# The state-space branch without GpSimd arithmetic, the gates' sigmoid in place, and the branch's tables begun seven steps later

## The chip, the core and the metric

The kernel runs on one core of a Trainium2 chip. The core has five engines that run side by side and wait for each other by semaphores: TensorE (PE; its weight loads are PEld), VectorE (DVE), ScalarE (ACT), GpSimd (POOL) and SyncE (SP). SP only issues transfers here; POOL issues some too. Each engine takes its instructions strictly in the order in which the program gives them, so an instruction that waits holds up all that stand behind it on its engine. The metric is the device time of one execution in microseconds.

## The reference, cut to what matters

One layer of a hybrid decoder for 1024 prompt tokens and 64 sample tokens (1088 columns in all; everything is fp32). The start of the layer is what the change touches:

```
h = rms_norm(x, norm_attn_g)
u, q_lat, kv_lat, k_rope, g_a, g_b = split(h @ w_in)        # 512, 384, 256, 32, 1024, 1024 columns
lb, bb = ssm_discretize(lam, log_dt, b)                     # 32 groups x 64 complex states
y, h_last = ssm_scan(u, h0, lb, bb, c, d)                   # h[t] = lb*h[t-1] + bb u[t];  y = Re(c h) + d u
z = gelu(y);  a_out = z * sigmoid(z @ w_glu)
b_out = latent attention (q_lat, kv_lat, k_rope)
x = x + (sigmoid(g_a)*(a_out @ w_branch_a) + sigmoid(g_b)*(b_out @ w_branch_b)) @ w_out
x = x + swiglu ffn(x);  x = x + gated per-layer embedding(x)
```

## The kernel before, in words

**Products.** Activations are stored transposed, 128 channels by 1088 tokens. Each fp32 product is made of three passes: both factors are split into a high and a low part, and `mm3` multiplies high by high, high by low and low by high. A tile of 128 output channels takes eight steps (one for each 128 input channels); a step is nine matmuls, three passes over three column chunks `CH`. A tile's three PSUM buffers are called `d`; there are six of them, so tile n+2 may begin only when tile n has been read out (`tag="d", bufs=6`).

**Weights.** `w_split` brings one unit of eight 128x128 blocks: SP loads `wr` (two buffers), ACT makes the high part `wh` (line 189), DVE the low part `wl` (line 190), and then SP is given the next `wr` load, which must wait until ACT and DVE have read the buffer. This is done at the first step of each tile, for the tile after it.

**Order of the work.** In `body`, the tiles of `w_in` come in this order: two tiles of `u`, which run with the norm's sums of squares (`sum_squares`) while x arrives; two more tiles of `u`; eight gates for `gbS` (called b0 to b7 here); eight for `gaS` (a0 to a7); two tiles of `kv`; one of `k_rope`; three of `q`. After its last step a tile is evacuated: `ev_gate` multiplies by the token's norm factor `Rb` on DVE (`gt`, line 402), takes the sigmoid on ACT (line 404) and stores by a transfer that POOL issues; `ev_u` does the like for `u`.

**Side work.** Everything else of this part is in generators that `tick` advances by one stage after each step: a stage is issued, and `yield n` says that the next comes n steps later. Two are spawned after the first two tiles: the rest of `stats` (token sums on PE, line 273; the inverse root `Rt` in eleven small DVE operations, lines 249 to 254; nine transposes on PE, line 288; `Rb` on ACT, line 290), five steps on; and `ssm_all`, `SW0` steps on. `ssm_all` runs `ssm_tables` (angles, exponentials, powers and the matrices `BB`, nearly all on DVE, some on POOL), then `ssm_block` four times (8 groups each). A block has these stages, with the steps between them in `WT`: `X` and `Y` (products of tables); `kp` in two halves (PE line 601, ACT line 603, sixteen transfers `M<-kp` on SP, line 605) with the transposes of `Y`; `Tc`, `Ts`, `rho`; `v` (PE line 638 in three groups that share two PSUM buffers, ACT line 639); the rotated scan (lines 648 to 671, DVE alone, ending in `Hp` and `fin`); `yb` (PE lines 680 and 681 in three groups, ACT line 682); and `ssm_tail`, whose gelu (line 702) comes much later. POOL does one of the two products in `X`, `Y`, `Tc` and `Ts`, and makes `rho`.

**Buffers.** All [128, 1088] tiles come from an arena of 38 slots: `S.free` puts a slot at the end of a list and `S.get` takes the first. A new tile so waits for the last reader of the slot's tile before; `v` and one `go` of each block have the slots of the two `kp`.

Of the kernel before, what the change touches and what calls it, by code (L numbers as in the profile page):

```python
# [14 lines left out]
AF = mybir.ActivationFunctionType  # L15
ALU = mybir.AluOpType
# [8 lines left out]
NT = SEQ + NS  # L25
# [16 lines left out]

N_SLOTS = 38
WRB = 2
SW0 = 4
WT = (8, 1, 7, 4, 9, 3, 1, 17, 11)
PVLAG = 3
WQ0 = 7
WS = 1
# [73 lines left out]
def body(ctx, tc, I, O):  # L123
    nc = tc.nc
    V, A, G, PE, SP = nc.vector, nc.scalar, nc.gpsimd, nc.tensor, nc.sync
# [87 lines left out]
    def spawn(gen, wait=0):  # L213
        side.append([gen, wait])
# [15 lines left out]
    S = Arena(sb, N_SLOTS)  # L230
# [73 lines left out]
    def sum_squares(k, x, acc):  # L304
        if k < 2:
            A.activation(acc[k], x, AF.Square)
        else:
            s = S.get([128, NT], name="sq")
            A.activation(s, x, AF.Square)
            (V if k % 2 == 0 else G).tensor_tensor(acc[k % 2], acc[k % 2], s, op=ALU.add)  # L310
            S.free(s)

    gaS = T(dr, [8, 128, NT], name="gaS")
# [27 lines left out]
    acc = [S.get([128, NT], name="acc") for _ in range(2)]  # L341
# [10 lines left out]
    Bab = S.get([128, 2, 32, 16], name="Bab")  # L352
# [45 lines left out]
    def ev_gate(m, dst):  # L398
        def ev(ps):
            t = S.get([128, NT], name="gt")  # L400
            for c, (c0, c1) in enumerate(CH):
                V.tensor_tensor(t[:, c0:c1], ps[c][:, :c1 - c0], Rb[:, c0:c1], op=ALU.mult)
            o = S.get([128, NT], name="go")
            A.activation(o, t, AF.Sigmoid)
            G.dma_start(dst[m], o)
            S.free(t, o)
        return ev

    def u_store(m, src):
# [18 lines left out]
    Cab = S.get([128, 2, 32, 16], name="Cab")  # L428
# [3 lines left out]
    def ssm_tables():  # L432
# [4 lines left out]
        def tiny(dt=F32):  # L437
            tn[0] += 1
            if dt is F32:
                return tp[(tn[0] - 1) // 32][:, (tn[0] - 1) % 32, :]  # L440
            return T(cp, [128, 32], dt, "tr")

        def tt(a, b, op, out=None):
            o = tiny() if out is None else out
            V.tensor_tensor(o, a, b, op=op)
            return o
# [48 lines left out]
        t1h = tiny()  # L495
        V.tensor_scalar(t1h, tot, 3072.0, 3072.0, op0=ALU.add, op1=ALU.subtract)
        t1l = tt(tt(tt(tt(s1, t1h, ALU.subtract), s2, ALU.add), s3, ALU.add), rest, ALU.add)

        b3 = [128, 32, 33]
        jb = jmul[:, None, :].to_broadcast(b3)  # L500
        ph = S.get(b3, name="ph")
# [6 lines left out]
            V.tensor_scalar(kk, ph, MAGIC, MAGIC, op0=ALU.add, op1=ALU.subtract)  # L508
            V.tensor_tensor(ph, ph, kk, op=ALU.subtract)

        G.tensor_tensor(ph, jb, t1h[:, :, None].to_broadcast(b3), op=ALU.mult)
        kk2 = S.get(b3, name="kk2")
        G.tensor_tensor(kk2, jb, t1l[:, :, None].to_broadcast(b3), op=ALU.mult)
        yield 3
        wrap()
        yield 1
# [3 lines left out]
        ph2 = S.get(b3, name="ph2")  # L520
        V.tensor_scalar(ph2, ph, 0.25, None, op0=ALU.add)
        V.tensor_scalar(kk2, ph2, MAGIC, MAGIC, op0=ALU.add, op1=ALU.subtract)
        G.tensor_tensor(ph2, ph2, kk2, op=ALU.subtract)
        yield 2
        A.activation(st, ph, AF.Sin, scale=TWO_PI)
        A.activation(ct, ph2, AF.Sin, scale=TWO_PI)
# [5 lines left out]
        pm, Pr, Pi = pw[:, 0], pw[:, 1], pw[:, 2]  # L532
        Prs, Pin, PiS = pw2[:, 0], pw2[:, 1], pw2[:, 2]
# [20 lines left out]
        frb = fr[:, :, None].to_broadcast(b16)  # L554
        f2b = f2[:, :, None].to_broadcast(b16)
        BB = S.get([128, 2, 32, 16], name="BB")
        tmp = S.get([128, 2, 32, 16], name="tmp")
        V.tensor_tensor(BB[:, 0], Bab[:, 0], frb, op=ALU.mult)
        G.tensor_tensor(tmp[:, 0], Bab[:, 1], f2b, op=ALU.mult)
        V.tensor_tensor(BB[:, 0], BB[:, 0], tmp[:, 0], op=ALU.add)  # L560
        G.tensor_tensor(BB[:, 1], Bab[:, 1], frb, op=ALU.mult)
        V.tensor_tensor(tmp[:, 1], Bab[:, 0], f2b, op=ALU.mult)
        V.tensor_tensor(BB[:, 1], BB[:, 1], tmp[:, 1], op=ALU.subtract)
        S.free(tmp, Bab, tp)
# [3 lines left out]
    def ssm_block(q):  # L568
        g0 = 8 * q
        gs = slice(g0, g0 + 8)  # L570
        Pr, Prs, Pin, PiS, pm, BB, st, ct = (SM[k] for k in ("Pr", "Prs", "Pin", "PiS", "pm", "BB", "st", "ct"))
# [5 lines left out]
        bx = [128, 4, 9, 16]  # L577
        for hf in range(2):
            hs = slice(g0 + 4 * hf, g0 + 4 * hf + 4)
            X2 = S.get(bx, name="X2")  # L580
            V.tensor_tensor(X[hf], Cab[:, 0, hs, None, :].to_broadcast(bx), Prs[:, hs, :, None].to_broadcast(bx), op=ALU.mult)
            G.tensor_tensor(X2, Cab[:, 1, hs, None, :].to_broadcast(bx), Pin[:, hs, :, None].to_broadcast(bx), op=ALU.mult)
            V.tensor_tensor(X[hf], X[hf], X2, op=ALU.add)
            S.free(X2)
        Y = S.get([128, 8, 8, 16], name="Y")
        Y2 = S.get([128, 8, 8, 16], name="Y2")
        by = [128, 8, 8, 16]
        G.tensor_tensor(Y, BB[:, 0, gs, None, :].to_broadcast(by), Pr[:, gs, 0:8, None].to_broadcast(by), op=ALU.mult)
        V.tensor_tensor(Y2, BB[:, 1, gs, None, :].to_broadcast(by), PiS[:, gs, 0:8, None].to_broadcast(by), op=ALU.mult)
        V.tensor_tensor(Y, Y, Y2, op=ALU.add)  # L590
        S.free(Y2)
        yield WT[0] + (WQ0 if q == 0 else 0)
        M1 = S.get([128, 8, 128], name="M1")
        Mi = S.get([128, 8, 128], name="Mi")
        for hf in range(2):
# [14 lines left out]
            for i in range(4):  # L610
                PE.transpose(p[:, i * 128:(i + 1) * 128], Y[:, 4 * hf + i].rearrange("p s c -> p (s c)"), ident)
            A.activation(Mi[:, 4 * hf:4 * hf + 4, :], p.rearrange("p (g c) -> p g c", g=4), AF.Copy)
            if WS & 2 and hf == 0:
                yield 1
        S.free(Y)
        yield WT[1]
        Tc = S.get([128, 8, 8, 16], name="Tc")
        Ts = S.get([128, 8, 8, 16], name="Ts")
        t1 = S.get([128, 8, 8, 16], name="t1")
        t2 = S.get([128, 8, 8, 16], name="t2")  # L620
        Ac, As = (x[:, gs, 9:17, None].to_broadcast(by) for x in (ct, st))
        Bc, Bs = (x[:, gs, None, 17:33].to_broadcast(by) for x in (ct, st))
        G.tensor_tensor(Tc, Ac, Bc, op=ALU.mult)
        V.tensor_tensor(t1, As, Bs, op=ALU.mult)
        V.tensor_tensor(Tc, Tc, t1, op=ALU.subtract)
        G.tensor_tensor(Ts, As, Bc, op=ALU.mult)
        V.tensor_tensor(t2, Ac, Bs, op=ALU.mult)
        V.tensor_tensor(Ts, Ts, t2, op=ALU.add)
        rho = S.get([128, 8, 128], name="rho")
        G.memset(rho, 0.0)  # L630
        G.tensor_tensor(rho[:, :, 1:128], rho[:, :, 1:128], pm[:, gs, 8:9].to_broadcast([128, 8, 127]), op=ALU.add)
        yield WT[2]
        v = S.get([128, 8, NCHK], name="v")
        for g in range(0, 8, 3):
# [7 lines left out]
        S.free(Mi)  # L642
        yield WT[3]
        f3 = lambda x: x.rearrange("p g a b -> p g (a b)")
# [27 lines left out]
        S.free(v, Tc, Ts, t1, t2, rho, Gs)  # L672
        yield WT[4]
        yb = S.get([128, 8, NCHK], name="yb")
        for g in range(0, 8, 3):
            n = min(3, 8 - g)
            p = m1()
            for i in range(n):
                o = p[:, i * NCHK:(i + 1) * NCHK]
# [5 lines left out]
        S.free(ug, M1, Hp, X)  # L685
        spawn(ssm_tail(q, yb), WT[5])
        yield WT[6]

    def ssm_tail(q, yb):
        for t in range(8):  # L690
            SP.dma_start(yS[q, t].rearrange("c g j -> c g j"), yb[t * 16:(t + 1) * 16])
        S.free(yb)
        yield WT[7]
        y = S.get([128, 8, NCHK], name="y")
        for g in range(8):
            SP.dma_start(y[g * 16:(g + 1) * 16], yS[q, :, :, g, :].rearrange("t c j -> c t j"))
        u = S.get([128, 8, NCHK], name="u")
        SP.dma_start(u, uS[q].rearrange("p (s j) -> p s j", s=8))
        yield WT[8]
        V.scalar_tensor_tensor(y, u, ssm_d[:, q:q + 1], y, op0=ALU.mult, op1=ALU.add)  # L700
        z = S.get([128, NT], name="z")
        A.activation(z.rearrange("p (j s) -> p s j", s=8), y, AF.Gelu_apprx_tanh)
        SP.dma_start(zS[q], z)
        S.free(y, u, z)
        done.append(q)
# [3 lines left out]
    def ssm_all():  # L709
        yield from ssm_tables()  # L710
        for q in range(4):
            yield from ssm_block(q)
        S.free(SM["st"], SM["ct"], SM["pw"], SM["pw2"], SM["BB"], spA, Cab)
        SP.dma_start(O["ssm"], fin)

    spawn(ssm_all(), SW0)
    for m in range(2, 4):
# [166 lines left out]
    for m in range(4):  # L884
# [4 lines left out]
        s = S.get([128, NT], name="ksq")  # L889
# [122 lines left out]
    for m in range(6):  # L1012
# [4 lines left out]
        s = S.get([128, NT], name="qsq")  # L1017
# [458 lines left out]
    bx = []  # L1476
# [41 lines left out]
    for m in range(4):  # L1518
# [5 lines left out]
        s = S.get([128, NT], name="s")  # L1524
# [26 lines left out]
    for m in range(8):  # L1551
        t = branch(m, ah, al, gaS, two[m] if m < 2 else None)
# [6 lines left out]
    for m in range(8):  # L1559
        ma = S.get([128, NT], name="ma")  # L1560
        SP.dma_start(ma, maS[m])
        t = branch(m, bh, bl, gbS)
# [8 lines left out]
    acc = []  # L1571
# [46 lines left out]
    ph, pl = [], []  # L1618
# [144 lines left out]
    for m in range(8):  # L1763
# [3 lines left out]
        t = S.get([128, NT], name="pe")  # L1767
# [171 lines left out]
    for m in range(8):  # L1939
        t = S.get([128, NT], name="t")  # L1940
# [160 lines left out]
```

## Time and profile before

| what | us |
|---|---|
| median of three runs (lowest to highest) | 2046.41 (2042.76 to 2052.85) |
| the profiled execution's own time | 2042.79 |
| its span, first to last instruction | 2041.0 |
| TensorE busy in the span | 1952.5 |

The span is what the trace shows; the execution's own time is 1.8 us more. The part of the program that the change touches runs in the first 342 us of the span. Busy time of TensorE is modelled and runs at the clock that was granted, so a stretch at a low clock counts as busy and is nevertheless lost time.

### The profile page before, as it was taken

The numbers are of one execution on the slowest core, as the hardware profiler recorded it, in microseconds if no ns is written. First come the engines' busy times: TensorE is split into PE (matmuls) and PEld (weight loads), VectorE is DVE, ScalarE is ACT, GpSimd is POOL, SyncE is SP. The second block draws the span as 40 slices with busy tenths as digits, with TensorE's granted clock in tenths as the row PEclk, the third lists the DMA queues.
The fourth block names the chain that finished last, engine by engine and source line by source line (L and its number), as shares of the span: only waits on it lengthen the run. The fifth ranks groups of instructions, "written<-read, shape, count | busy, mean of one in ns | idle before, by whom it ended". The sixth has DMA issues, their size and how long they took to land.

```text
span 2041.0 us, 34073 instructions
## 1 busy us (share of the span) xinstructions
PE 1952.5 (96%) x12912; PEld 1890.0 (93%) x12912; DVE 1288.8 (63%) x2073; ACT 866.4 (42%) x1954; POOL 321.8 (16%) x304
## 2 busy tenths in 40 slices
PE   7899999999999989989999999999999999999998
PEld 7898999976778989989999998999999999999998
DVE  6967675565887898887554477555555554444543
ACT  4121322465777877776312254333333331211321
POOL 2212220224332033333200000000000000000212
PEclk9899999999998999999999999999999999999999
DMA  4224433424323665543654352212212153222132
GB/s 181 75 96 119 138 114 117 131 96 109 74 56 105 191 176 157 149 140 129 221 211 150 134 208 90 96 64 78 82 64 96 64 205 130 86 85 75 64 118 88
DMA packets 108518, 242.90 MB, mean 119 GB/s; under 512 B 15673, under 2 KB 64186, under 8 KB 108354
## 3 DMA queue, kind: packets, MB, share of 16 engines
q1 hardware_dynamic: 102674, 218.85, 34.0%
q0 software_dynamic: 5680, 21.87, 2.8%
q8 instruction: 102, 1.67, 0.3%
q14 instruction: 62, 0.51, 0.1%
HBM read 180.02 MB, written 53.50 MB: 114 GB/s over the span
## 4 chain that ended last, share of the span: by engine, by line
PE 50%; DVE 2%; ACT 1%; issue 1%; DMA 1%; POOL 0%; POOLq 0%; ACTq 0%; DVEq 0%
PE d L244 28%; PE d L1823 20%; PE m L1301 1%; PE b L1401 0%; DVE o L1718 0%; PE a L1400 0%; DVE w L235 0%; ACT w L234 0%; DMA gate<-gbS 0%; POOL t L1951 0%; DMA hS<-G 0%; PE m L273 0%; ACT t L1950 0%; ACT pe L1769 0%; DVE t L1949 0%
## 5 line engine op out<-in xcount | busy, mean ns | idle before, releaser
L1823 PE MATMUL d<-o,w 128*128 128x272 f32 x3528 | 444.7, 288 | 5.5 <-ACT P L1869 4.6
L1823 PEld LDWEIGHTS d<-o,w 128*128 128x128 f32 x3528 | 443.6, 189 | 6.6 <-ACT P L1869 5.3
L1400 PE MATMUL a<-wuA,T 128*128 128x256 f32 x768 | 217.7, 295 | 2.5 <-DVE T L235 2.5
L1401 PE MATMUL b<-WB,T 128*128 128x320 f32 x768 | 214.9, 316 | 0.0
L244 PE MATMUL d<-xh,wh 128*128 128x360 f32 (+2 forms) x816 | 189.6, 338 | 11.4 <-ACT wh L189 7.7
L244 PE MATMUL d<-xl,wh 128*128 128x360 f32 (+2 forms) x816 | 185.5, 333 | 1.6 <-DVE xl L238 1.6
L244 PE MATMUL d<-xh,wl 128*128 128x360 f32 (+2 forms) x816 | 184.5, 332 | 0.0
L190 DVE TENSOR_TENSOR wl<-wr,wh 128x1024 fp32r<-128x1024 f32 x83 | 135.9, 1638 | 70.1 <-ACT wh L189 70.1
L189 ACT ACTIVATE wh<-wr 128x1024 fp32r<-128x1024 f32 x83 | 87.4, 1055 | 176.8 <-PE d L244 162.6
L244 PEld LDWEIGHTS d<-xh,wh 128*128 128x128 f32 x816 | 145.0, 194 | 14.8 <-ACT wh L189 7.7
L1400 PEld LDWEIGHTS a<-wuA,T 128*128 128x128 f32 x768 | 149.5, 195 | 3.4 <-DVE T L235 3.0
L1401 PEld LDWEIGHTS b<-WB,T 128*128 128x128 f32 x768 | 148.5, 193 | 0.2 <-ACT s L1426 0.2
L244 PEld LDWEIGHTS d<-xl,wh 128*128 128x128 f32 x816 | 145.9, 193 | 2.7 <-DVE xl L238 2.7
L244 PEld LDWEIGHTS d<-xh,wl 128*128 128x128 f32 x816 | 145.5, 192 | 0.1
L1910 DVE TENSOR_TENSOR x<-d,x 128x368 f32<-128x368 f32 x144 | 68.0, 528 | 114.5 <-PE d L244 114.5
L1584 POOL TENSOR_TENSOR acc<-acc,sq 128x1088 f32<-128x1088 f32 x4 | 10.7, 2671 | 698.0 <-ACT sq L1582 698.0
L244 PE MATMUL d<-hh,wl 128*128 128x368 f32 x528 | 115.4, 326 | 0.0
L244 PE MATMUL d<-hh,wh 128*128 128x368 f32 x528 | 115.4, 326 | 0.0
L244 PE MATMUL d<-hl,wh 128*128 128x368 f32 x528 | 115.4, 326 | 0.0
L235 DVE TENSOR_TENSOR w<-rg,w 128x512 fp32r<-128x512 f32 x63 | 43.4, 692 | 101.0 <-ACT w L234 101.0
L235 POOL TENSOR_TENSOR nat<-rawN,nat 128x512 fp32r<-128x512 f32 x60 | 81.3, 1358 | 131.6 <-ACT nat L234 111.2
L1425 DVE TENSOR_REDUCE ms<-sqd 128x8 f32<-128x512 f32 x128 | 84.9, 683 | 21.4 <-ACT sqd L1424 19.8
(462 smaller groups left out, 3902.7 us busy)
## 6 DMA issues: line engine op xcount, KB each, us to landing
wr<-in_wstream_dram SPq DMA_DIRECT2D x83, 512.0 KB, 4.1
rawT<-in_recT_dram SPq DMA_DIRECT2D x128, 208.0 KB, 2.5
rawN<-in_recN_dram SPq DMA_DIRECT2D x128, 128.0 KB, 2.3
hx<-hS SPq DMA_DIRECT2D x22, 544.0 KB, 6.4
hS<-G SPq DMA_DIRECT2D x21, 544.0 KB, 3.0
rg<-in_wstream_dram SPq DMA_DIRECT2D x21, 512.0 KB, 4.8
ru<-in_wstream_dram SPq DMA_DIRECT2D x21, 512.0 KB, 5.6
x<-in_xT_dram SPq DMA_DIRECT2D x16, 544.0 KB, 5.6
```

Source lines behind the costliest of these rows:

```text
L189: A.activation(h, r, AF.Copy)
L190: V.tensor_tensor(l, r, f(h), op=ALU.subtract)
L235: (leng or V).tensor_tensor(lo, x, f(hi), op=ALU.subtract)
L244: PE.matmul(ps[c][:, :c1 - c0], a, b[:, c0:c1], start=first and j == 0, stop=last and j == 2)
L1301: PE.matmul(o[:, 0:n], st, mv[:, j, 0:n], start=i == 0 and j == 0, stop=i == NBLK - 1 and j == 1)
L1400: PE.matmul(pa, st, wuA[:, k, w], start=first, stop=k == 1 and j == 2)
L1401: PE.matmul(p[:, 0:320], st, WB[k][:, w, wc], start=first, stop=False)
L1425: V.tensor_reduce(ms[:, i], sq.rearrange("p a (h d) -> p (a h) d", d=64), axis=AX.X, op=ALU.add)
L1584: e.tensor_tensor(a, a, s, op=ALU.add)
L1823: PE.matmul(bank[bk][c], w[:, wj, p, :], ops[i][p][:, xj, sl[c]], start=bool(opens and p == 0 and j == 0), stop=p == 3 and j == 2, skip_gr ...
L1910: V.tensor_tensor(xr[m][:, c0:c1], ps[c][:, :c1 - c0], xr[m][:, c0:c1], op=ALU.add)
```

## The change

Five things are done. (1) Arithmetic of the state-space branch and of the first norm moves from POOL (`G`) to DVE (`V`), operation by operation; `rho`, which POOL made by a clear and an addition, is made by a POOL clear of one column and an ACT copy. (2) A gate's sigmoid is written over its input, so that `ev_gate` takes one slot and not two. (3) `SW0` goes from 4 to 11, so that the tables begin seven steps later. (4) `WT[0]` goes from 8 to 5 and `WT[2]` from 7 to 6. (5) A `yield 1` is added after each half of `X` and one between `Tc` and `Ts`. The steps between `kp` and `v`, `v` and the scan, and the scan and `yb` stay as they were (10, 4 and 9 steps); a block as a whole takes 31 steps and not 32.

```diff
-SW0 = 4
-WT = (8, 1, 7, 4, 9, 3, 1, 17, 11)
+SW0 = 11
+WT = (5, 1, 6, 4, 9, 3, 1, 17, 11)
...
-            (V if k % 2 == 0 else G).tensor_tensor(acc[k % 2], acc[k % 2], s, op=ALU.add)
+            V.tensor_tensor(acc[k % 2], acc[k % 2], s, op=ALU.add)
...
-            o = S.get([128, NT], name="go")
-            A.activation(o, t, AF.Sigmoid)
-            G.dma_start(dst[m], o)
-            S.free(t, o)
+            A.activation(t, t, AF.Sigmoid)
+            G.dma_start(dst[m], t)
+            S.free(t)
...
-        G.tensor_tensor(ph, jb, t1h[:, :, None].to_broadcast(b3), op=ALU.mult)
+        V.tensor_tensor(ph, jb, t1h[:, :, None].to_broadcast(b3), op=ALU.mult)
         kk2 = S.get(b3, name="kk2")
-        G.tensor_tensor(kk2, jb, t1l[:, :, None].to_broadcast(b3), op=ALU.mult)
+        V.tensor_tensor(kk2, jb, t1l[:, :, None].to_broadcast(b3), op=ALU.mult)
...
-        G.tensor_tensor(ph2, ph2, kk2, op=ALU.subtract)
+        V.tensor_tensor(ph2, ph2, kk2, op=ALU.subtract)
...
-        G.tensor_tensor(tmp[:, 0], Bab[:, 1], f2b, op=ALU.mult)
+        V.tensor_tensor(tmp[:, 0], Bab[:, 1], f2b, op=ALU.mult)
...
-        G.tensor_tensor(BB[:, 1], Bab[:, 1], frb, op=ALU.mult)
+        V.tensor_tensor(BB[:, 1], Bab[:, 1], frb, op=ALU.mult)
...
-            G.tensor_tensor(X2, ...)
+            V.tensor_tensor(X2, ...)
             V.tensor_tensor(X[hf], X[hf], X2, op=ALU.add)
             S.free(X2)
+            yield 1
...
-        G.tensor_tensor(Y, ...)
+        V.tensor_tensor(Y, ...)
...
-        G.tensor_tensor(Tc, Ac, Bc, op=ALU.mult)
+        V.tensor_tensor(Tc, Ac, Bc, op=ALU.mult)
         V.tensor_tensor(t1, As, Bs, op=ALU.mult)
         V.tensor_tensor(Tc, Tc, t1, op=ALU.subtract)
-        G.tensor_tensor(Ts, As, Bc, op=ALU.mult)
+        yield 1
+        V.tensor_tensor(Ts, As, Bc, op=ALU.mult)
...
-        G.memset(rho, 0.0)
-        G.tensor_tensor(rho[:, :, 1:128], rho[:, :, 1:128], pm[:, gs, 8:9].to_broadcast([128, 8, 127]), op=ALU.add)
+        G.memset(rho[:, :, 0:1], 0.0)
+        A.activation(rho[:, :, 1:128], pm[:, gs, 8:9].to_broadcast([128, 8, 127]), AF.Copy)
```

How the order moves is shown at three places. The first is DVE around the norm's inverse root. Before, its instructions (lines 249 to 254) stand behind the first stage of the tables (`tiny`):

```order
L445 TENSOR_TENSOR tiny_399<-tiny_399 128x32 x4
L496 TENSOR_SCALAR tiny_399<-tiny_399 128x32
L445 TENSOR_TENSOR tiny_399<-tiny_399 128x32 x4
L249 TENSOR_SCALAR sm_469<-m_459 128x9
L250 TENSOR_SCALAR Rt_68<-sm_469 128x9
L252 TENSOR_TENSOR sm_470<-Rt_68 128x9
```

In the changed kernel they stand behind two low parts of weights, right after the norm's sums of squares:

```order
L310 TENSOR_TENSOR acc_93<-acc_93,sq_294 128x1088
L296 TENSOR_TENSOR acc_92<-acc_92,acc_93 128x1088
L190 TENSOR_TENSOR wl_325<-wr_133,wh_324 128x1024
L190 TENSOR_TENSOR wl_358<-wr_151,wh_357 128x1024
L249 TENSOR_SCALAR sm_418<-m_408 128x9
L250 TENSOR_SCALAR Rt_68<-sm_418 128x9
```

What moved is the whole first stage of the tables: it now follows the inverse root and the evacuation of three tiles of `u`.

The second place is DVE at the end of the tables. Before, the last `BB` operation is followed by the evacuation of the fourth tile of `u`, a low part of weights, `X` and `Y` of the first block, and only then by the evacuation of gate b0 (`gt`):

```order
L563 TENSOR_TENSOR BB_677<-BB_677,tmp_678 128x512
L412 TENSOR_TENSOR u_685<-d_544,Rb_318 128x46x8
L412 TENSOR_TENSOR u_685<-d_545,Rb_318 128x45x8
L412 TENSOR_TENSOR u_685<-d_546,Rb_318 128x45x8
L190 TENSOR_TENSOR wl_694<-wr_361,wh_693 128x1024
L581 TENSOR_TENSOR X_726<-Cab_352,pw_56_617 128x576
L583 TENSOR_TENSOR X_726<-X_726,X_68_728 128x576
L581 TENSOR_TENSOR X_727<-Cab_352,pw_56_617 128x576
L583 TENSOR_TENSOR X_727<-X_727,X_69_732 128x576
L589 TENSOR_TENSOR Y_71_737<-BB_677,pw_56_617 128x1024
L590 TENSOR_TENSOR Y_736<-Y_736,Y_71_737 128x1024
L402 TENSOR_TENSOR gt_795<-d_690,Rb_318 128x368
```

In the changed kernel b0 is evacuated right after `BB`, and `X` and `Y` come behind it:

```order
L562 TENSOR_TENSOR BB_754<-BB_754,tmp_755 128x512
L402 TENSOR_TENSOR gt_771<-d_633,Rb_318 128x368
L402 TENSOR_TENSOR gt_771<-d_634,Rb_318 128x360
L402 TENSOR_TENSOR gt_771<-d_635,Rb_318 128x360
L190 TENSOR_TENSOR wl_781<-wr_495,wh_780 128x1024
L580 TENSOR_TENSOR X_804<-Cab_352,pw_57_694 128x576
L581 TENSOR_TENSOR X_69_806<-Cab_352,pw_57_694 128x576
L582 TENSOR_TENSOR X_804<-X_804,X_69_806 128x576
```

What moved: the fourth tile of `u` is now evacuated earlier, inside the tables, and gate b0 before `X` and `Y`.

The third place is ACT in the blocks. Before, in every block, a gate's sigmoid and the weights' high part come just ahead of `kp` (here the first block, b1's sigmoid):

```order
L404 ACTIVATE go_887<-gt_883 128x1088
L189 ACTIVATE wh_893<-wr_697 128x1024
L603 ACTIVATE kp_910<-m_912 16x4x128
L612 ACTIVATE Mi_909<-m_935 128x512
L603 ACTIVATE kp_941<-m_943 16x4x128
L612 ACTIVATE Mi_909<-m_966 128x512
```

In the changed kernel nothing stands ahead of `kp` at that place; in the third block, a pair of sigmoids with their high parts stands between `v` and `yb`, the later pair just ahead of `yb`:

```order
L640 ACTIVATE v_2115<-m_2126 128x272
L403 ACTIVATE gt_2139<-gt_2139 128x1088
L189 ACTIVATE wh_2148<-wr_1904 128x1024
L403 ACTIVATE gt_2257<-gt_2257 128x1088
L189 ACTIVATE wh_2266<-wr_2044 128x1024
L683 ACTIVATE yb_2308<-m_2309 128x408
L683 ACTIVATE yb_2308<-m_2317 128x408
L683 ACTIVATE yb_2308<-m_2325 128x272
```

What moved is the place of each block's stages among the gates' evacuations. Counting the steps of a tile from 1 to 8, `kp`, `v` and `yb` came after steps 1, 3 and 8 in every block; now they come after steps 7, 1 and 6 in the first, 6, 8 and 5 in the second, 5, 7 and 4 in the third, and 4, 6 and 3 in the fourth. The first GpSimd arithmetic of the program is now line 816 (815 before), in the rotary part of the keys, and the setting-up of GpSimd that stood ahead of its first addition at line 310 stands there.

## Rows read from the trace of the kernel before

**Rows 1.** The page: busy time and share of the span of each engine.

```profile
PE 1952.5 (96%) x12912; PEld 1890.0 (93%) x12912; DVE 1288.8 (63%) x2073; ACT 866.4 (42%) x1954; POOL 321.8 (16%) x304
```

**Rows 2.** TensorE's waits, first 500 us: in total, times, longest.

```profile
PE m L638 <- ACT v L639: 8.7, 4, 3.2
...
PE m L288 <- DVE Rt L254: 5.3, 1, 5.3
PE m L601 <- ACT kp L603: 4.8, 3, 2.1
PE d L244 <- DVE u L412: 3.1, 1, 3.1
...
PE d L244 <- DVE xl L238: 1.6, 3, 1.2
PE m L680 <- ACT yb L682: 1.4, 2, 0.7
```

**Rows 3.** Stretches: length; busy PE, PEld, DVE, ACT, POOL; PEclk; DMA.

```profile
37.70:102.70 65.00, 56.56 (x317) 55.10 (x316) 56.80 (x122) 12.18 (x15) 17.27 (x13) 0.89 0.26 83
102.70:341.70 239.00, 223.92 (x1388) 217.71 (x1387) 169.30 (x162) 63.61 (x79) 51.58 (x52) 0.97 0.41 117
40.90:98.84 57.94, 49.50 (x274) 48.04 (x273) 53.96 (x118) 8.06 (x9) 16.68 (x12) 0.88 0.24 76
50.03:53.97 3.94, 0.00 (x0) 0.00 (x0) 3.60 (x12) 0.00 (x0) 2.00 (x1) 0.84 0.00 0
89.80:98.84 9.04, 9.04 (x46) 9.04 (x45) 8.73 (x7) 0.00 (x0) 5.18 (x3) 0.78 0.71 181
253.00:266.40 13.40, 13.40 (x83) 13.40 (x82) 12.97 (x15) 0.00 (x1) 0.00 (x0) 1.00 0.33 75
60.71:72.55 11.84, 11.84 (x73) 11.84 (x73) 11.56 (x14) 4.30 (x5) 3.59 (x3) 1.00 0.41 153
```

**Rows 4.** Timeline of DVE, first 33 us: start, length, operation.

```profile
22.00 7.17 DVE L238 SCALAR_TENSOR_TENSOR xl<-x,gains,xh 128x1088 fp32r<-128x1088 f32 x2
...
30.30 1.34 DVE L238 SCALAR_TENSOR_TENSOR xl<-x,gains,xh 128x1088 fp32r<-128x1088 f32 x1
```

**Rows 5.** Groups of DVE, 40.9 to 98.84 us: busy us, mean ns, idle before.

```profile
L457 DVE TENSOR_SCALAR fe<-pw 128x288 f32<-128x288 f32 x1 | 2.5, 2468 | 0.0
...
L250 DVE TENSOR_SCALAR Rt<-sm 128x9 int32<-128x9 int32 x1 | 2.0, 1991 | 0.0
L560 DVE TENSOR_TENSOR BB<-BB,tmp 128x512 f32<-128x512 f32 x1 | 1.5, 1530 | 1.0 <-POOL tmp L559 1.0
```

**Rows 6.** Line 445, 40 to 98 us: shortest, median, longest in ns.

```profile
L445 DVE TENSOR_TENSOR tiny<-tiny x14: 184/192/1878, 45.1 to 81.6; 128x32 f32<-128x32 f32 x14
```

**Rows 7.** Groups of DVE, 102.7 to 341.7 us: busy us, mean ns, idle before.

```profile
L190 DVE TENSOR_TENSOR wl<-wr,wh 128x1024 fp32r<-128x1024 f32 x17 | 50.5, 2973 | 50.1 <-ACT wh L189 50.1
...
L624 DVE TENSOR_TENSOR t<-st 128x1024 f32<-128x1024 f32 x4 | 11.8, 2950 | 0.0
...
L625 DVE TENSOR_TENSOR Tc<-Tc,t 128x1024 f32<-128x1024 f32 x4 | 4.9, 1226 | 0.4
```

**Rows 8.** Timelines of SP's queue and of ACT in the first block.

```profile
112.81 0.35 SPq L178 DMA_DIRECT2D wr<-in_wstream_dram  x1
113.26 10.41 SPq L605 DMA_DIRECT2D M<-kp  x16
...
126.06 0.91 ACT L639 ACTIVATE v<-m 128x408 f32<-128x408 f32 x2 [3.06 <-DMA M<-kp]
```

**Rows 9.** Timelines of PE and of ACT, 45 to 102 us.

```profile
45.13 2.06 PE L273 MATMUL m<-cst,acc 128*128 128x2 f32 x18
...
101.31 1.04 ACT L189 ACTIVATE wh<-wr 128x1024 fp32r<-128x1024 f32 x1
```

**Rows 10.** POOL: line 310's set-up, and the timeline at 378 us.

```profile
L310 POOLq MODIFY_POOL_CONFIG  x2: 11/11/11, 0.8 to 0.8; - x2
...
378.46 2.94 POOL L815 TENSOR_TENSOR kpr<-kpr,rope 48x1088 f32<-48x1088 f32 x1 [2.59 <-DMA rope<-in_ropek_dram]
```

More of the change, by code (lines that the diff above doesn't have):

```diff
@@ L581, in ssm_block @@
             V.tensor_tensor(X[hf], Cab[:, 0, hs, None, :].to_broadcast(bx), Prs[:, hs, :, None].to_broadcast(bx), op=ALU.mult)
-            G.tensor_tensor(X2, Cab[:, 1, hs, None, :].to_broadcast(bx), Pin[:, hs, :, None].to_broadcast(bx), op=ALU.mult)
+            V.tensor_tensor(X2, Cab[:, 1, hs, None, :].to_broadcast(bx), Pin[:, hs, :, None].to_broadcast(bx), op=ALU.mult)
             V.tensor_tensor(X[hf], X[hf], X2, op=ALU.add)
             S.free(X2)
+            yield 1
         Y = S.get([128, 8, 8, 16], name="Y")
@@ L587, in ssm_block @@
         by = [128, 8, 8, 16]
-        G.tensor_tensor(Y, BB[:, 0, gs, None, :].to_broadcast(by), Pr[:, gs, 0:8, None].to_broadcast(by), op=ALU.mult)
+        V.tensor_tensor(Y, BB[:, 0, gs, None, :].to_broadcast(by), Pr[:, gs, 0:8, None].to_broadcast(by), op=ALU.mult)
         V.tensor_tensor(Y2, BB[:, 1, gs, None, :].to_broadcast(by), PiS[:, gs, 0:8, None].to_broadcast(by), op=ALU.mult)
```

## Prediction, made before the changed kernel was run

> **What bounds the kernel now.** I read the page's engine line first: TensorE is busy for 1952.5 of 2041.0 us [rows 1], so only time in which it waits, or runs at a lower clock, can be won. The change touches the first 342 us and leaves TensorE's order behind them as it is; the sum is therefore made from the waits there [rows 2] and from the clock of two stretches [rows 3]: 0.89 of full speed (which is 2.4 GHz) from 37.70 to 102.70 us, and 0.97 from 102.70 to 341.70. The lost clock comes to 65.00 x 0.11 = 7.2 us and 239.00 x 0.03 = 7.2 us. I take each loss of clock to follow one of the long waits, and so price a dip at half of 7.2 in the first stretch (two long waits, 5.3 and 3.1 us, 3.6 for each) and at a quarter of 7.2 in the second (four blocks, 1.8 for each).
>
> What holds TensorE there? In the tables it is DVE: from 40.90 to 98.84 us it is busy for 53.96 of 57.94 us [rows 3], a chain that starts with the tables, contains the norm's inverse root, and ends at b0's evacuation. In the blocks DVE is busy for 169.30 of 239.00 us only, yet TensorE waits 8.7 us for `v` and 4.8 for `kp` [rows 2].
>
> The reader should next compare like operations of DVE, since some take several times as long as others of the same shape. Low parts of x take 7.17 us for two and 1.34 for one [rows 4]. An operation on 128x9 takes 1.99 us, one on 128x288 takes 2.47, and a 128x512 addition 1.53 after 1.0 of idling [rows 5]; line 445 takes 0.18 us as a rule and 1.88 once [rows 6]. In the blocks 17 low parts of weights take 50.5 us, a mean of 2.97, beside 1.23 for a product of the same shape, and the product at line 624 takes 2.95 [rows 7]. The long ones lie where POOL computes: at 50.03 to 53.97 us, the inverse root, POOL shows one operation of 2.00 us [rows 3]. I take it that DVE's two-input operations stand still while POOL works, and that the excess goes when POOL's arithmetic goes.
>
> The Trainium skill, SBUF — State Buffer, section SBUF: two separate sides, says that DVE and GpSimd share a port pair as an exclusive lock, so that the later one fully blocks; the long rows agree with that, except that the 128x288 and 128x9 rows have a single tensor input, which the page's list names only for a performance mode. By that rule the excess goes wholly; without it the rival "VectorE is simply full" below would be the forecast.
>
> One long operation in the blocks does more than cost DVE time. SP loads the next `wr` only when `wl` has been read, and the sixteen `M<-kp` stand behind that load: `wr` goes at 112.81, `M<-kp` takes 10.41 us from 113.26, and ACT idles 3.06 us for it before it writes `v` at 126.06 into `kp`'s old slot [rows 8]. So POOL's arithmetic holds DVE, DVE holds SP, SP holds ACT, ACT holds TensorE.
>
> **The change, part by part.**
>
> Sums of squares: three additions of 1.28 us go to DVE, but 7.17 - 2 x 1.34 = 4.5 us of excess goes [rows 4]. TensorE waits 1.6 us for `xl` in three places [rows 2]; I take two of them as gone: 1.4 us.
>
> Inverse root: the token sums end at 45.13 + 2.06 = 47.2 us [rows 9], after that gain at 45.8. The inverse root took 3.94 us [rows 3]; its one long operation falls from 1.99 to about the shortest of line 445, 0.18, so 2.1 us are left, and `Rt` is ready at 47.9 instead of 54.0. TensorE's 5.3 us wait for it [rows 2] falls to about 1.
>
> Tables: `Rb` follows some 1.7 us later, 49.6 us, and now the same DVE chain begins there. Its length is 57.94, less 3.94 (the inverse root, now ahead), less 9.04 (`X` and `Y`, now behind b0) [rows 3], less the excess of 5.75 (line 445 1.7; line 457 2.2, its normal time put at 0.3; line 560 0.85 and 1.0) [rows 5, 6], plus what comes from POOL: three operations of 128x1056 and two of 128x512, by line 625's 1.226 for 1024 columns [rows 7] 3 x 1.26 + 2 x 0.61 = 5.0, less 1.3 that DVE idled for one of them: about 48 - 5.75 + 5.2 = 44.4. b0 is read out at 94.0 and no more at 98.84. From there to the weights of b2 it took until 101.31 + 1.04 = 102.35 [rows 9], 3.5 us, since ACT's high part stands behind b0's sigmoid. So b2 can begin at 97.5.
>
> TensorE could begin it earlier. Before, it was there at 102.70 with 5.3 + 3.1 us of waits and 7.2 us of low clock behind it; with 1.4 won earlier, a wait of 1 left, and 1.3 us of low clock kept, it would be there at 102.7 - 1.4 - 4.3 - 3.1 - 5.9 = 88. **A new wait of about 9.5 us stands at b2**, and a dip of 3.5 behind it. The front gains 102.7 - 97.5 - 3.5 = 1.7 us, not 14.7.
>
> Blocks: the waits of before are 8.7 + 4.8 + 1.4 = 14.9 us [rows 2], with the clock 22.1. DVE loses 50.5 - 17 x 1.23 = 29.6 and 4 x (2.95 - 1.23) = 6.9 us of excess, and receives per block three products of 1.23 and two of 128x576, 0.7 each: 20.4 in all [rows 7]. It ends with less work than before, so it does not become the bound. `wl` no longer holds SP, so `M<-kp` starts some 4 us earlier against ACT's 3.06 of idling: `v`'s wait goes, but for the first block, where `v` comes after step 1 and stands behind a sigmoid and a high part of 1.04 [rows 9]: 1.4 us, and 0.1 in each other. `kp` comes after steps 7, 6, 5 and 4, where ACT has no sigmoid ahead of it: 0. `yb` now comes after steps 6, 5, 4 and 3. The scan's chain is 13.4 us long, nine steps of 11.84 / 8 = 1.48 us [rows 3]; gates whose read-out stands behind that chain bring their sigmoids and high parts late. In the third block such a pair stands just ahead of `yb`: the chain's 13.4 us, 1.4 for a read-out, 1.1 for the sigmoid and 1.04 for the high part keep ACT until about 17 us after the scan's start; TensorE comes to `yb` after nine steps, 13.3 us, and two PSUM buffers carry it 1.5 us further: a wait of 2.2 us, and a dip of 1.8. In the fourth block `Hp` is late by about 0.9. In all 1.7 + 2.2 + 0.9 = 4.8, and 1.8 of clock: the blocks gain 22.1 - 6.6 = 15.5 us.
>
> Costs put at nothing: the `rho` copy on ACT (1016 columns a partition, about 1.04 us by the high part [rows 9]) lies in ACT's idle time ahead of `v`; if that cover is gone, four times 1.04. The sigmoid in place costs what it did. POOL's clear is on one column. The set-up of POOL that stood at 0.8 us, 11 ns twice, comes now ahead of line 815's operation at 378.46 us, where POOL idles 2.59 us for a transfer [rows 10]. Its price is not shown: nothing at the lower end, and at the upper the whole time until the first addition there, 15.8 us, which would push the rotary keys and cost TensorE 9 to 12 us after the cover. I take 11 ns, the only row of it.
>
> **Sum.** 1.7 + 15.5 = 17.2 us. The profiled execution's time of 2042.79 becomes 2025.6; the median of the runs is 3.6 us above it, and I put the forecast between, at 2027.
>
> **The rivals.**
>
> A. VectorE is simply full, and its long operations are not POOL's doing. For it: DVE is busy 93% of the tables' stretch, and it receives 5.0 us there. Against it: one shape has two times, and the long ones lie beside POOL's. Then the chain is 5.75 longer, `Rt` 1.8 later, b2 begins at 105 with its dip: a loss of 5.8 at the front, and the blocks gain 3 to 5 only from the new phases (DVE's 20.4 us come on top): 2040 to 2046.
> The Trainium skill, Perfetto Trace Analysis, section Optimizing Scalar/DVE Operations, advises that when DVE is saturated some work may go to Scalar or even GpSimd, and this change goes the other way; it adds that the shared port can undo the benefit, which is what the rows bear out.
>
> B. ScalarE's queue takes the place of the removed waits. If in all blocks `v` and `yb` meet a sigmoid and a high part, four times 1.4 + 2.2 and the four dips of 1.8 stay: 21.6 of the 22.1, and the time is about 2040. The place of the stages in the order speaks for it in blocks one and three only.
>
> C. The change does not do what it says: `v` waits for the 10.41 us in which SP issues `M<-kp` [rows 8], not for when it starts. Then 8.7 us and the dips stay: 2039. Against it: ten steps of 1.48 us lie between `kp` and `v`, 14.8 us.
>
> D, slower: POOL's set-up in mid-program. DVE's rotary addition waits for it, the keys' split on ACT stands behind that, and the next tiles' read-outs behind both, so TensorE waits. It takes about 5 us of cover and 17 of gain before it decides for slower: a set-up over 32 us. The 11 ns row speaks against it, the gap of 15.8 us for only half of that.
>
> **How the numbers follow.** 10 us, 0.5%, is about what a measurement of this kernel can tell from no change. My forecast (gain 10 to 25) has 0.62; A 0.12, B 0.12, C 0.08, D 0.06. Faster: my case, and a part of B and C that ends beyond 10 us: 0.68. Same: the rest of A, B and C, 0.26. Slower 0.06. The range goes down to 2012, where b2's wait is not there (another 9 to 13 us), and up to 2043, which holds B, C and half of A. My case alone gives 2014 to 2035.
>
> **What would show it.** Right: no waits for `xl` but one; a wait for `Rt` of about 1 us; line 190 at 1.2 us throughout; one wait near 9 us between 88 and 98 us, at gate b2; waits for `v` of 2 us in all, none for `kp`, one of 2 for `yb` in the third block; the clock from 102 to 342 us at 0.99. Wrong: long operations of DVE with no POOL beside them (A); waits behind sigmoids in every block (B); `M<-kp` early and `v` still late (C); a gap on POOL ahead of line 816 of more than some us (D). The most doubtful term is b2's wait.

## Result, and the profile after

The changed kernel takes 2025.16 us (median of 4 runs, 2021.56 to 2026.51) against 2048.76 us before (4 runs, three of them those of the table ahead of the prediction). The ratio is 0.9891, with a 95% interval of 0.9871 to 0.9911: 1.1% faster. 2027 was forecast. The profiled execution took 2025.91 us.

The page's engine line, then TensorE's waits in the first 500 us (in total, times, longest), which answer to [rows 1, 2]:

```profile
PE 1946.8 (96%) x12912; PEld 1886.3 (93%) x12912; DVE 1263.3 (62%) x2101; ACT 871.2 (43%) x1958; POOL 256.7 (13%) x272
```

```profile
PE d L244 <- ACT wh L189: 16.2, 2, 8.6
...
PE m L681 <- ACT yb L683: 1.5, 1, 1.5
...
PE m L639 <- ACT v L640: 1.0, 1, 1.0
PE m L288 <- DVE Rt L254: 0.7, 1, 0.7
...
PE m L682 <- DVE Hp L665: 0.6, 1, 0.6
...
PE d L244 <- DVE xl L238: 0.2, 1, 0.2
```

The waits for `kp` and for `u` are gone. Of the two waits in the first row, 7.6 us are for the program's first weights, which were waited for before too, and 8.6 are the new wait at b2. The chain at the front, on the timelines of DVE, ACT and TensorE:

```profile
45.22 0.17 DVE L249 TENSOR_SCALAR sm<-m 128x9 f32<-128x9 f32 x1 [6.23 <-PE m L273]
45.42 0.17 DVE L250 TENSOR_SCALAR Rt<-sm 128x9 int32<-128x9 int32 x1
...
77.84 0.31 DVE L456 TENSOR_SCALAR fe<-pw 128x288 f32<-128x288 f32 x1
...
92.71 1.42 DVE L402 TENSOR_TENSOR gt<-d,Rb 128x368 f32<-128x368 f32 x3
```

```profile
95.17 1.04 ACT L189 ACTIVATE wh<-wr 128x1024 fp32r<-128x1024 f32 x1
```

```profile
96.26 1.27 PE L244 MATMUL d<-xh,wh 128*128 128x368 f32 x3 [8.63 <-ACT wh L189]
```

The operations of 1.99 and 2.47 us [rows 5] now take 0.17 and 0.31 (the second, line 457 before, is line 456 here). The read-out of b0 begins at 92.71, the weights of b2 are ready at 96.2, and TensorE waits 8.63 us for them. The stretches (columns as in [rows 3]) and DVE's groups from 102.7 to 341.7 us [rows 7]:

```profile
37.70:102.70 65.00, 55.40 (x331) 54.57 (x331) 52.74 (x128) 10.19 (x12) 2.87 (x5) 0.92 0.25 87
102.70:341.70 239.00, 235.59 (x1506) 230.12 (x1505) 157.62 (x198) 73.63 (x89) 12.34 (x31) 1.00 0.42 121
```

```profile
L190 DVE TENSOR_TENSOR wl<-wr,wh 128x1024 fp32r<-128x1024 f32 x17 | 20.8, 1224 | 37.4 <-ACT wh L189 37.4
...
L624 DVE TENSOR_TENSOR t<-st 128x1024 f32<-128x1024 f32 x4 | 4.9, 1218 | 0.0
```

Every long operation is gone, and the clock, at 0.97 in the blocks before, is full there. As a mark behind the branch I use the first matmul of the keys' norm (its row: shortest, median, longest ns, first and last start), before and after:

```profile
L797 PE MATMUL m<-cst,ckv x2: 271/286/300, 369.0 to 373.1; 128*128 128x128 f32 x2
```

```profile
L798 PE MATMUL m<-cst,ckv x2: 270/284/299, 346.0 to 350.3; 128*128 128x128 f32 x2
```

There the gain is 23.0 us; at the end of the span it is 2041.0 - 2024.1 = 16.9. What became of 6 us is the question of two of the experiments.

### The profile page after: what moved, and what is told of

It is laid out like the page before. It is cut to its first block, busy times and chain, and to the rows that moved or that the text cites. A ratio compares the mean times of both kernels' runs of the same rounds, so it can differ in the third digit from the quotient of the medians.

```text
span 2024.1 us, 34045 instructions
## 1 busy us (share of the span) xinstructions
PE 1946.8 (96%) x12912; PEld 1886.3 (93%) x12912; DVE 1263.3 (62%) x2101; ACT 871.2 (43%) x1958; POOL 256.7 (13%) x272
## 4 chain that ended last, share of the span: by engine, by line
PE 41%; issue 11%; DVE 2%; DMA 1%; ACT 1%; POOL 0%; POOLq 0%; SPq 0%; ACTq 0%; DVEq 0%
PE d L1824 20%; PE d L244 19%; PE m L1302 1%; PE b L1402 0%; PE a L1401 0%; DMA gate<-gaS 0%; DVE w L235 0%; ACT w L234 0%; DVE o L1719 0%; DMA peS<-pe 0%; DMA hS<-G 0%; POOL t L1952 0%; ACT t L1951 0%; POOL peS L1771 0%; DVE t L1950 0%
## 5 line engine op out<-in xcount | busy, mean ns | idle before, releaser
L190 DVE TENSOR_TENSOR wl<-wr,wh 128x1024 fp32r<-128x1024 f32 x83 | 106.2, 1281 | 60.4 <-ACT wh L189 60.4
```

Source lines behind the costliest of these rows:

```text
L190: V.tensor_tensor(l, r, f(h), op=ALU.subtract)
```

## The experiments

"Mark" is the start of that first matmul (369.0 us before, 346.0 after). Ratios are to runs of the kernel before on the same chip.

| kernel | median us (runs) | ratio, 95% | mark us |
|---|---|---|---|
| arithmetic alone | 2024.18 (4) | 0.9890, 0.9860 to 0.9921 | 345.1 |
| order and buffers alone | 2036.15 (8) | 0.9963, 0.9941 to 0.9986 | 358.5 |
| arithmetic of the blocks alone | 2026.12 (4) | 0.9897, 0.9881 to 0.9914 | 350.7 |
| before, weights' load later | 2037.43 (7) | 0.9960, 0.9937 to 0.9983 | 360.4 |
| GpSimd probe | 2022.22 (1) | | 352.5 |
| sums of squares on GpSimd | 2018.70 (1) | | 348.3 |
| sigmoid in a second tile | 2026.51 (4) | 0.9896, 0.9866 to 0.9926 | 347.2 |
| changed kernel again | 2024.38 (4) | 0.9891, 0.9875 to 0.9907 | 346.6 |
| before, second trace | 2051.52 (1) | | 369.5 |
| first stage of the tables early | 2013.00 (4), 2013.13 (5) | 0.9860, 0.9832 to 0.9888; 0.9853, 0.9830 to 0.9875 | 337.7, 339.9 |

**Does GpSimd hold DVE?** Useless GpSimd work in the changed kernel, ahead of `Tc`:

```diff
+        if q % 2 == 0:
+            for _ in range(3):
+                G.tensor_tensor(Y2, Ac, Bc, op=ALU.mult)
+        else:
+            for _ in range(6):
+                G.memset(Y2, 0.0)
```

> The changed kernel with useless GpSimd work added ahead of Tc in each block, about 5.8 us each time: three products of 128x1024 in the first and third block, six clears of 128x1024 (no tensor read) in the second and fourth. Theory that DVE's operations stand still while GpSimd computes on tensors: in blocks one and three a DVE operation beside the products takes 3 to 6 us in place of 1.2, in two and four all keep 1.2. Rival that any GpSimd instruction holds DVE: long ones in all four blocks. Rival that GpSimd doesn't matter: none. Time within 8 us of the changed kernel.

Timelines of POOL (blocks one and two) and of DVE (block one, then two):

```profile
115.76 7.82 POOL L624 TENSOR_TENSOR Y<-ct 128x1024 f32<-128x1024 f32 x3
...
180.17 6.05 POOL L627 MEMSET Y<- 128x1024 f32 x6
```

```profile
115.81 3.02 DVE L190 TENSOR_TENSOR wl<-wr,wh 128x1024 fp32r<-128x1024 f32 x1 [2.88 <-ACT wh L189]
118.76 2.99 DVE L629 TENSOR_TENSOR Tc<-ct 128x1024 f32<-128x1024 f32 x1
121.67 2.99 DVE L630 TENSOR_TENSOR t<-st 128x1024 f32<-128x1024 f32 x1
124.70 1.23 DVE L631 TENSOR_TENSOR Tc<-Tc,t 128x1024 f32<-128x1024 f32 x1
...
181.47 1.22 DVE L629 TENSOR_TENSOR Tc<-ct 128x1024 f32<-128x1024 f32 x1
182.61 1.22 DVE L630 TENSOR_TENSOR t<-st 128x1024 f32<-128x1024 f32 x1
```

Three products of GpSimd lengthen three operations of DVE, one each, to 3.0 us, and take 2.6 each themselves in the mean; the fourth is normal. Six clears over 6.05 us lengthen none. So it is GpSimd's products that hold DVE, and not its being busy. The clears read no tensor and do no arithmetic, so the probe doesn't tell which of the two counts.

In the kernel before, the turns were not one for one. Timelines of DVE and of POOL in its first block:

```profile
107.11 5.67 DVE L190 TENSOR_TENSOR wl<-wr,wh 128x1024 fp32r<-128x1024 f32 x1 [2.17 <-ACT wh L189]
```

```profile
107.80 1.95 POOL L623 TENSOR_TENSOR Tc<-ct 128x1024 f32<-128x1024 f32 x1
109.73 1.97 POOL L626 TENSOR_TENSOR Ts<-st,ct 128x1024 f32<-128x1024 f32 x1
```

One low part lasted until both products were over. The mean of 2.97 us [rows 7] hides this: ten of the 17 low parts took 1.2 us and seven 5.1 to 5.7, each of these beside two or three products of GpSimd in a row. Why the engines alternate in the probe and not here stays open.

In block one of the probe the late read-out of a gate also brought back a wait for `v` of 4.9 us; in block three, where the products held no low part, none came.

**Which part gains?** First the arithmetic alone, with the steps and buffers of before (`SW0 = 4`, `WT = (8, 1, 7, ...)`, no new yields, sigmoid in its own tile):

> The kernel before with GpSimd's arithmetic moved to DVE and ACT and nothing else: the tables begin after 4 steps, the steps between the stages are those of before, the sigmoid has its own tile. Theory (DVE stands still while GpSimd computes): every low part of weights takes 1.2 us from 102 us on, the waits for v (8.7 us before) fall under 1 us, those for kp (4.8) and yb (1.4) stay, since they come from the places of the stages behind the gates' sigmoids; the norm's root is ready near 49 us and TensorE waits 2 us for it. Time 2028 to 2036, so most but not all of the gain. Rival (VectorE was simply full): DVE's 20 us more of work leave the time at 2044 or above.

Then all the rest, with GpSimd's arithmetic left in place:

> The changed kernel with GpSimd's arithmetic put back: tables after 11 steps, new steps between the stages, sigmoid in place. Theory: long low parts of weights of over 4 us remain in each block and the waits for v stay at 5 to 9 us, those for kp go to about 0; the wait at gate b2 is 10 to 12 us since the tables' chain is longer. Time 2038 to 2045. Rival (the places of the stages, not GpSimd, make the gain): 2025 to 2030.

TensorE's waits in the first 345 us with the arithmetic alone, and then with order and buffers alone (in the first row of these, one of the two waits is that of the program's first weights, 7.4 us, and the longest is b2's):

```profile
PE d L244 <- DVE u L412: 5.7, 1, 5.7
PE m L680 <- ACT yb L682: 2.2, 3, 0.7
PE m L288 <- DVE Rt L254: 1.8, 1, 1.8
PE m L601 <- ACT kp L603: 0.9, 2, 0.5
```

```profile
PE d L244 <- ACT wh L189: 18.5, 2, 11.1
PE d L244 <- DVE wl L190: 3.1, 1, 3.1
PE m L639 <- ACT v L640: 2.8, 1, 2.8
PE m L681 <- ACT yb L683: 2.0, 2, 1.4
```

The arithmetic alone gains the whole (its ratio can't be told from the change's). I had expected `kp` to keep its 4.8 us and the time to stay at 2028 or above; `kp` keeps 0.9 and the time is 2024.18. Order and buffers alone gain 0.4%, more than I had expected (2036.15, not 2038 to 2045): they too take away most of `kp`'s wait and of `v`'s (2.8 us left, where I had expected 5 to 9), but pay with 11.1 us at b2, because the tables' chain is both later and held. So the two parts remove the same waits, and their gains don't add.

The arithmetic of the blocks alone (`X2`, `Y`, `Tc`, `Ts`, `rho`; sums and tables stay on GpSimd):

> The kernel before with only the blocks' arithmetic (X2, Y, Tc, Ts, rho) taken from GpSimd; the sums of squares and the tables stay as before, and so do all steps. Theory: the front keeps its waits (root 5.3, u 3.1, xl 1.6 us), the blocks lose theirs (v and kp together under 2 us, from 13.5): 14 to 18 us of gain, 2027 to 2032. Rival (the front is what counts): under 8 us of gain, above 2037.

The front kept its waits (root 5.3 us, `u` 3.9), `v`'s went, `kp` kept 0.9 and `yb` 2.2; the mark is 18.3 us earlier. The blocks are four fifths of the gain at the mark. The time (2026.12) can't be told from the changed kernel's on the same chip (2024.38), so what the front adds is seen at the mark alone.

**The chain from the low part to `v`.** The kernel before, with the next load of weights given to SP four steps later:

```diff
-            w_load()
+            if not 2 <= u < 22:
+                w_load()
...
+        if i == 4 and nxt["load"] < nxt["split"] + WRB and u < 21:
+            w_load()
```

> The kernel before, GpSimd's arithmetic left in place, with one thing changed: the next load of weights is given to SP four steps later in the tile, so that the sixteen M<-kp no longer stand behind a load that waits for the low part. Theory of the prediction (long low part holds SP, SP holds M<-kp, that holds v): M<-kp of the first block starts near 109 us in place of 113.3, the waits for v fall from 8.7 us to under 3, the low parts stay long, the waits for kp stay at 4 to 5; time 2030 to 2040. Rival (v waits for DVE's lateness itself, through the gate's read-out and its sigmoid on ACT): the waits for v stay above 6 us and the time at 2042 or above.

SP's queue, and TensorE's waits:

```profile
108.18 10.55 SPq L608 DMA_DIRECT2D M<-kp  x16
118.83 6.63 SPq L178 DMA_DIRECT2D wr<-in_wstream_dram  x3
```

```profile
PE m L604 <- ACT kp L606: 4.8, 3, 2.1
...
PE m L641 <- ACT v L642: 2.6, 2, 2.3
```

`M<-kp` starts at 108.18 in place of 113.26 [rows 8], `v`'s wait falls from 8.7 to 2.6 us, and `kp`'s stays to the tenth, though the 17 low parts still take 50.6 us. That a load queued ahead of `M<-kp` made `v` late is shown; the edit is worth 0.4% by itself.

**Smaller parts.** Three sums of squares back on GpSimd:

> The changed kernel with three additions of the sums of squares back on GpSimd. Theory: the low parts of x beside them take over 3 us, TensorE's waits for xl return (1.4 us in all, 0.2 in the changed kernel), the first two tiles end 2 us later, and the rest of the branch moves with them, with a new wait at gate b2 between 7 and 10 us; time 1 to 3 us above the changed kernel. Rival: the tables' chain, which sets b2, doesn't feel it, and nothing is lost.

The waits for `xl` are 1.6 us again and the wait at b2 8.6; the mark comes 2.3 us later than in the changed kernel's first trace and 1.7 later than in its second. The waits for `xl` are as priced (1.4 us), the whole term is somewhat more. Its one time, 2018.70, is nevertheless below the changed kernel's, against the 1 to 3 us more that I had expected: this is the scatter that is taken up below.

The sigmoid in a tile of its own:

> The changed kernel with the gate's sigmoid written to a tile of its own again. Theory (in place costs and gives nothing, since buffers are never short here): the same waits of TensorE to within 1 us, 2022 to 2028. Rival (the second slot makes a later tile wait for its slot): a wait of over 2 us that the changed kernel doesn't have, 2028 or above.

Waits in the blocks as in the changed kernel to a tenth, but 10.0 us at b2 in place of 8.6. ACT's timeline there:

```profile
94.73 1.28 ACT L404 ACT_TABLE_LOAD   x1 [15.63 <-DVE gt L402]
96.02 1.11 ACT L404 ACTIVATE go<-gt 128x1088 f32<-128x1088 f32 x1
```

The sigmoid's table load, 1.28 us, now waits for the gate's read-out; in the changed kernel it stood at 78.58 us, where ACT idled. So in place gave something that I had not priced, 1.4 us at this one spot. It is no rule of two tiles: in the kernel before, which has two as well, the same load stood at 73.44 us, where ACT idled. Why the wait stands ahead of the load in one order and behind it in another isn't shown. The effect on the time can't be told from none.

**Where did 6 us go behind the branch?**

> The changed kernel itself, beside the next run on the same chip, and for a second profile. Theory (the 6 us that it gave back behind the branch are a matter of where low-clock stretches fall, not of the change): the gain at the end of the branch is again 23 us, and what is lost or won behind it differs from the first profile by some us; time 2021 to 2027. Rival (given back by the change itself): again 6 us given back between 418 and 640 us.

> The kernel before, unchanged, for a second trace of it. Theory (the first trace of it was one of its faster executions, because little low clock fell behind the branch): the branch ends at the same time as in the first trace, within 1 us, and the low clock behind it, up to 950 us, costs 27 us or more in place of 23.9; span near 2046. Rival (the changed kernel itself loses clock there): again 23 to 24 us, span near 2041.

The same 80 us of work in four traces, 71 us behind the mark (columns as in [rows 3]): before, before again, changed, changed again:

```profile
440.00:520.00 80.00, 72.32 (x339) 53.87 (x339) 52.73 (x91) 46.39 (x92) 33.80 (x42) 0.94 0.46 130
```

```profile
440.00:520.00 80.00, 73.72 (x303) 54.41 (x302) 48.10 (x74) 40.70 (x77) 32.03 (x35) 0.83 0.41 121
```

```profile
417.00:497.00 80.00, 74.34 (x314) 55.96 (x314) 48.26 (x80) 42.91 (x83) 30.37 (x35) 0.83 0.44 126
```

```profile
417.00:497.00 80.00, 74.30 (x314) 55.79 (x313) 48.27 (x79) 42.51 (x81) 30.96 (x35) 0.83 0.42 125
```

The changed kernel lost there as much as in its first trace, against what I expected of it; but the second trace of the kernel before, equal to the first up to the mark (369.5), has 0.83 there too and ends at 2049.7 us. So the loss need not be the change's: the first trace of before had been one of its better executions, 6 us under the median of 2048.76, and the gain of the medians, 23.6 us, is that at the mark. Why this stretch falls at 0.94 in some executions and 0.83 in others stays open.

**A version that beats both.** The changed kernel with the tables' first stage issued ahead of the norm's root:

```diff
-SW0 = 11
+SW0 = 4
...
         ct = S.get(b3, name="ct")
-        yield 1
+        yield 8
```

> The changed kernel with the first stage of the tables (7.4 us of small DVE operations) issued 7 steps earlier, ahead of the norm's root, where DVE idled 6.2 us; every later stage keeps its place. Theory (the 8.6 us wait at gate b2 is the end of DVE's chain, tables then b0): the root is ready 1 us later, the wait at b2 falls by about 6 us to 2 to 3 us, the dip of the clock behind it shrinks, and the time is 2012 to 2020. Rival (the small operations delay the root, and TensorE waits there instead): a wait of over 5 us for the root, time 2023 to 2030.

> The changed kernel with the tables' first stage ahead of the norm's root, beside the changed kernel on the same chip. Theory (the wait at gate b2 and the low clock behind it are worth 7.4 and 5 us): 9 to 14 us faster than the changed kernel. Rival (half of the earlier difference was chance): 3 to 7 us faster.

TensorE's waits from 35 to 103 us, and the stretches:

```profile
PE m L288 <- DVE Rt L254: 1.8, 1, 1.8
PE d L244 <- ACT wh L189: 1.2, 1, 1.2
```

```profile
37.70:102.70 65.00, 61.71 (x380) 60.08 (x380) 56.86 (x134) 12.70 (x14) 4.20 (x8) 1.00 0.27 90
102.70:341.70 239.00, 234.83 (x1500) 229.53 (x1498) 160.06 (x202) 73.32 (x89) 12.13 (x32) 1.00 0.43 122
```

The wait at b2 falls from 8.6 to 1.2 us, the root costs 1.1 more, and the low clock in the first stretch goes. These are rows of the first trace; in the second the wait at b2 is 0.9 us, but the clock there is 0.97 and not 1.00. On the same chip it takes 2013.13 us against the changed kernel's 2024.38: 11 us less. Only 6.7 to 8.3 us of it are there at the mark (346.6 against 339.9, 346.0 against 337.7). Behind it both traces have a clock of 0.94 in the same 80 us as above (408.7 to 488.7 and 410.9 to 490.9 us), where both traces of the changed kernel have 0.83. The kernel before had the one as well as the other, so whether this part of the 11 us belongs to the edit is not shown. The wait at b2 was the end of DVE's chain, as forecast, and `SW0 = 11` had put 7.4 us of it there that DVE could have done while it idled 6.23 us for the token sums.

## Why the prediction was right, step by step

- **Long operations are GpSimd's doing**: shown by the probe; DVE's groups fell to 20.8 and 4.9 us. Rival A (VectorE full) is out: DVE's work fell although it received all.
- **Front.** The wait for `xl` falls by 1.4 us, as priced; the root's first operation starts at 45.22 (45.8 forecast), its wait is 0.7 us (1); b0 is read out at 92.71 (94.0); b2 begins at 96.26 (97.5) after 8.6 us (9.5). From 102.71 the start of b2 moved by 6.4 us, of which the clock behind it takes some 2.2: 4.2 gained against 1.7 forecast. Of the 2.5 us between them, 1.2 come from the chain, whose sum is taken up below, and 1.3 from the dip, priced at 3.5. The prediction took all time at the low clock as lost. By that count the first stretch now loses 65.00 x 0.08 = 5.2 us, but 8.63 x 0.34 = 2.9 of them lay in the wait itself, where TensorE had nothing to do (the wait, then the 6.44 us behind it, columns as in [rows 3]):

```profile
87.63:96.26 8.63, 0.00 (x1) 0.00 (x1) 6.30 (x17) 2.05 (x2) 0.53 (x1) 0.66 0.00 0
96.26:102.70 6.44, 6.44 (x27) 6.44 (x28) 6.37 (x8) 0.00 (x0) 0.00 (x0) 0.66 0.72 224
```

- **Blocks.** `v` 1.0, `yb` 1.5, `Hp` 0.6, `kp` 0: 3.1 us in place of 4.8, each in the block for which it was forecast (`v` in the first, `yb` in the third, `Hp` in the fourth), and no low clock where 1.8 were put. So some 19 us were gained, and 15.5 forecast. Rivals B and C didn't come: no sigmoid stood ahead in every block, and `M<-kp`, once early, was no bound.
- **What was wrong in it.** `kp`'s 4.8 us were credited to the new places of the stages. The arithmetic alone does that as well, so the places are not needed for it: the sigmoids still stand ahead of `kp` there, and they came too late only while DVE's low parts were long (with these kept and only the load moved, `kp` waits 4.8 us as before). Either part is enough: order and buffers alone leave 0.6 us. The length of DVE's chain is added up wrongly: its own terms, 57.94 - 3.94 - 9.04 - 5.75 + 5.0 - 1.3, make 42.9 us and not 44.4. With 42.9, b0 would have been put at 92.5, b2 at 96.0 and the front's gain at 3.2; measured were 92.71, 96.26 and 4.2. And I made the sum against an execution that was fast by chance: the gain of medians is 23.6 us, like the 23.0 at the mark and above the sum of 17.2. The sum was some 6 us too small and its starting point some 6 us too low; that the time came out within 2 us is luck in this part.
- **GpSimd's set-up** (rival D): no price. These are POOL's rows at line 816; its wait is again that for `rope`, 2.47 us, as 2.59 in [rows 10]. The last row is the probe's, where no wait could hide a delay: its first product starts at 115.76 us, right behind the set-up.

```profile
L816 POOLq MODIFY_POOL_CONFIG  x2: 12/12/12, 353.0 to 353.0; - x2
```

```profile
355.51 2.86 POOL L816 TENSOR_TENSOR kpr<-kpr,rope 48x1088 f32<-48x1088 f32 x1 [2.47 <-DMA rope<-in_ropek_dram]
```

```profile
L624 POOLq MODIFY_POOL_CONFIG  x2: 37/37/37, 115.7 to 115.7; - x2
```

## What to carry to other kernels

Compare like shapes within one engine: where an operation has two durations, look what another engine does beside the long one, and price what stands in the queues behind it (here a load, then sixteen transfers, then `v`) before pricing the operation. Moving work to the busier engine can shorten both. Two edits that remove the same wait are not worth their sum, so try each alone; and mark the gain at the end of the touched part, since a single trace of either kernel can be several us off behind it.

## What the hardware did that was not expected

- DVE and GpSimd hold each other when both work on tensors. In the probe they take turns operation by operation, DVE at 3.0 us in place of 1.22 and GpSimd at 2.6 in the mean, where the kernel before had 1.9 to 2.0. In that kernel one DVE operation lasted over two or three GpSimd products in a row (5.1 to 5.7 us). Clears on GpSimd cost DVE nothing.
- DVE operations with one tensor input are held as well: 128x9 took 1.99 us beside GpSimd [rows 5] and 0.17 without, 128x288 2.47 and 0.31. On these shapes the prediction had a reservation. Without GpSimd, operations with one input go at nearly twice the rate of those with two, as DVE's timeline of the changed kernel shows; whether this is the performance mode of which the prediction speaks, no run here shows.

```profile
66.16 0.70 DVE L507 TENSOR_SCALAR kk<-ph 128x1056 f32<-128x1056 f32 x1
66.89 1.26 DVE L508 TENSOR_TENSOR ph<-ph,kk 128x1056 f32<-128x1056 f32 x1
```

- One program, equal to within 0.5 us up to 369 us, ran 80 us of later work at a mean clock of 0.94 in one execution and 0.83 in another, and ended 8.7 us apart (spans of 2041.0 and 2049.7).
